# The first k-tile of a decoder trunk: its products term by term, and other idle matmuls ahead of them

## The chip, the cores and the metric

The kernel runs on one core of one Trainium2 chip. The metric is the device time of one execution in microseconds (us), as a median over runs. PE is TensorE, DVE VectorE, ACT ScalarE, POOL GpSimd and SP SyncE. PEld is PE's loading of weights, which overlaps its matmuls.

## The reference

The computation is a decoder trunk of two layers on 256 tokens of width 1024, in float32. Layer 0 mixes tokens by block attention with 16 heads of 64; with 256 tokens there is one block, so it is plain causal attention. Layer 1 mixes by dilated windows with 12 heads. Each mixer is followed by a dense MLP of width 4096 with a squared ReLU, and each of the four sub-layers by a layer norm.

```python
h = x
for i in range(DEPTH):                      # DEPTH = 2
    mix = moba_attention(...) if i % 2 == 0 else dilated_attention(...)
    h = layer_norm(DEEPNORM_ALPHA * h + mix, ln_mix_g[i], ln_mix_b[i])
    h = layer_norm(DEEPNORM_ALPHA * h + sq_relu_mlp(h, mlp_w_in[i], mlp_w_out[i]), ln_mlp_g[i], ln_mlp_b[i])
```

What matters here is the very first product, `qkv = x @ w_qkv` of layer 0, and of it the columns of the queries and keys.

## The kernel before, in words

Every float32 operand is split into a high and a low part of the type fp32r. A product is then three matmuls ("terms"): high weights by high tokens (term 0), high weights by low tokens (term 1), low weights by high tokens (term 2). ACT or DVE makes the high part (`whi`, `xs` part 0), DVE subtracts it from the source for the low part (`wlo`, `xs` part 1); both are done by `split` (lines 349 to 357).

The first block of work computes six weight tiles of 128 query and key columns (`NFIRST = 6`) over a contraction of 1024, which is cut into eight k-tiles of 128. One k-tile is a `Stage`: its 256 token columns and its 768 weight columns lie side by side in one array in DRAM, `xw0`, and are loaded together. `STAGE_PARTS` (line 54) says in how many parts a stage is loaded and split. The first k-tile has the tokens, then three parts of the weights: tile 0, tiles 1 and 2, tiles 3 to 5. SP loads the tokens with tile 0, ACT's queue loads the other five tiles. DVE makes the high part of tile 0, ACT the high parts of the other two. The second k-tile has two parts, tiles 0 and 1 and tiles 2 to 5; the later ones have fewer.

`Stage.mms(ps, j, term)` adds one matmul of weight tile `j` and one term: the weights are stationary (128x128), 256 token columns move. Two tiles share a PSUM bank, so the block uses three banks, `first_ps`. A k-tile has 18 of these matmuls, the block 144. The loop over the stages that the diff touches adds them, for the first k-tile in an order of its own: the three terms of tile 0 first, then term by term the tiles 1 to 5.

Ahead of the block stand idle matmuls: products of constant ones in bf16 into a bank that nobody reads. `WARM` (line 60) lists their column counts. One more idle matmul is added behind the first product of the first k-tile; it reads the same operands as that product, so that it cannot come sooner.

```python
def idle(n, reads=()):
    ones = nc.const_aps.tensor
    op("PE", n / 2400, lambda: mm(idle_ps.t[:, :n], ones(1.0, [P, P], BF16), ones(1.0, [P, n], BF16), True, True),
       list(reads), [idle_ps])
for n in WARM:
    idle(n)
```

The order on each engine is not the order of the program text. `op` only records an operation with its engine, an estimated cost, its reads and its writes. `Plan.order` (line 163) goes over the list twice. The first pass, in the order of the text, gives each operation a due time from PE's progress and the estimated arrivals of the loads. The second pass places operations engine by engine: of those that can start first, the one that is due first. SP's loads keep the order of the text. `Plan.emit` then writes the instructions in the order found. All matmuls show line 360 in the profile, the splits 351, 353 and 356, the loads 347; rows are told apart by their tiles.

Of the kernel before, what the change touches and what calls it, by code (L numbers as in the profile page):

```python
# [47 lines left out]
NFIRST = 6  # L48
# [8 lines left out]
    ((2, NFIRST), ("ACT", "ACT"), ((0, 1, "SP"), (2, 2, "SP"))),  # L57
    ((NFIRST,), ("ACT",), ((0, 1, "SP"),)),
)
WARM = (512,) * 6 + (384,)  # L60

# [51 lines left out]
class Plan:  # L115
# [16 lines left out]
    def op(self, eng, cost, fn, reads=(), writes=(), xfer=0.0, early=0.0, ahead=0.0):  # L132
        o = Op()
        o.n, o.eng, o.cost, o.fn, o.xfer = len(self.ops), eng, cost, fn, xfer
        o.early, o.ahead = early, ahead
        o.preds, o.succs, o.bufs = set(), [], set()
        for group, is_write in ((reads, False), (writes, True)):
            for item in group:
                b, key = item if isinstance(item, tuple) else (item, None)
                o.bufs.add(b)  # L140
                for k, st in b.state.items():
                    if key is None or k is None or k == key:
                        if st[0] is not None:
                            o.preds.add(st[0])
                        if is_write:
                            o.preds.update(st[1])
                st = b.state.setdefault(key, [None, []])
                if is_write:
                    if key is None:
                        b.state = {None: [o, []]}  # L150
                    else:
                        st[0], st[1] = o, []
                else:
                    st[1].append(o)
        o.preds.discard(o)
        for p in o.preds:
            p.succs.append(o)
        for b in o.bufs:
            b.left += 1
        self.ops.append(o)  # L160
        return o
# [129 lines left out]
def tile_trunk(  # L291
# [37 lines left out]
    def mk(shape, dt, tag, bufs, space=None):  # L329
        uid[0] += 1  # L330
        return plan.buf(Bufs(space or sb, bufs), shape, dt, tag, bufs, f"{tag}_{uid[0]}")

    def psum(tag):
        return mk([P, 512], F32, tag, 4, ps_pool)
# [24 lines left out]
    def mm(out_ap, lhsT, rhs, start, stop):  # L359
        nc.tensor.matmul(out_ap, lhsT, rhs, start=start, stop=stop)  # L360
# [16 lines left out]
    xs = [mk([P, 4, 2, S], F32R, f"xs{i}", 1) for i in range(2)]  # L377
# [73 lines left out]
    def idle(n, reads=()):  # L451
        ones = nc.const_aps.tensor
        op(
            "PE", n / 2400, lambda: mm(idle_ps.t[:, :n], ones(1.0, [P, P], BF16), ones(1.0, [P, n], BF16), True, True),
            list(reads), [idle_ps],
        )

    for n in WARM:
        idle(n)
# [140 lines left out]

    first_ps = [psum("acc") for _ in range(NFIRST // 2)]
    for st in stages:

        todo = sorted((st.kt + j > 0, term, j) for term in range(3) for j in range(NFIRST))
        for _, term, j in todo:
            st.mms(first_ps[j // 2], j, term)
            if st.kt == term == j == 0:
                idle(512, [(st.hi, (0, 1)), (xs[0], (0, 0, 0))])


    turns = {"score": 0, "prob": 0}
# [680 lines left out]
```

## Time and profile before

| | |
|---|---|
| time, median of 3 runs | 562.04 us (560.03, 562.04, 562.15) |
| profiled execution | 562.25 us |
| its span | 560.4 us |
| PE busy | 552.2 us (99% of the span) |
| PEld busy | 472.2 us (84%) |
| DVE busy | 412.3 us (74%) |
| ACT busy | 302.4 us (54%) |
| bytes moved by DMA | 105.60 MB, mean 188 GB/s |

A row of the timeline gives the start and the length in microseconds from the span's beginning, the engine, the line, the operation, what it writes and reads, the shape and how many instructions of a kind follow each other. The length of a merged row reaches to the end of its last instruction, and rows of matmuls overlap, so the pace of matmuls is read from the distance between starts. A bracket gives the idle time ahead of a row and what ended it.

### The profile page before, as it was taken

The page shows a single profiled execution, that of the slowest core. Times are in us where ns is not written, and L with a number is a line of the kernel's source. Part 1 is how long each engine was busy: PE and PEld are TensorE (multiplying, and loading weights), DVE is VectorE, ACT ScalarE, POOL GpSimd, SP SyncE. Part 2 cuts the span into 40 slices and gives each one's busy share as a digit, 9 for nine tenths or more (in the row PEclk, how much of TensorE's full clock was granted, in tenths as well). Part 3 has the DMA queues.
Part 4 walks back from the last instruction along what each step waited for, and adds up shares of the span by engine and source line. Part 5 has one row for each costly group of instructions (what it writes and reads, how often), then busy time and mean ns, then how long its engine had stood idle before and what let it go on. Part 6 is the DMA issues. An engine that isn't in the chain of part 4 may idle for free.

```text
span 560.4 us, 8584 instructions
## 1 busy us (share of the span) xinstructions
PE 552.2 (99%) x3235; PEld 472.2 (84%) x3235; DVE 412.3 (74%) x726; ACT 302.4 (54%) x491; POOL 8.6 (2%) x13
## 2 busy tenths in 40 slices
PE   9999999999999999999999999999999999999995
PEld 7988888888888888888888889888888888888884
DVE  6599999897764854855879999889848548458446
ACT  6367798258455455455534567545654554555400
POOL 0000000000000000000000000010000000000001
PEclk9999999999999999999999999999999999999998
DMA  8976145638885855647336535525877456463001
GB/s 334 404 280 207 51 167 198 235 112 299 268 272 157 245 171 186 225 153 223 123 141 216 198 118 185 169 94 181 300 233 252 163 187 224 149 227 113 1 0 75
DMA packets 30137, 105.60 MB, mean 188 GB/s; under 512 B 3345, under 2 KB 4113, under 8 KB 30097
## 3 DMA queue, kind: packets, MB, share of 16 engines
q1 hardware_dynamic: 29808, 104.48, 55.5%
q8 instruction: 25, 0.41, 0.3%
q10 hardware_dynamic: 288, 0.59, 0.3%
q14 instruction: 16, 0.12, 0.1%
HBM read 104.01 MB, written 1.05 MB: 187 GB/s over the span
## 4 chain that ended last, share of the span: by engine, by line
PE 98%; DMA 1%; DVE 0%; POOLq 0%; DVEq 0%; ACT 0%; issue 0%
PE acc L360 59%; PE tp L360 36%; PE tp L690 3%; DMA raw<-in_xw_dram 1%; POOLq L1286 0%; DVE tok L556 0%; DVEq L1286 0%; DVE bst L824 0%; ACT xs L351 0%; DVE mv L802 0%; DVE rstd L803 0%; POOLq L805 0%
## 5 line engine op out<-in xcount | busy, mean ns | idle before, releaser
L356 DVE TENSOR_TENSOR wlo<-raw,whi 128x1024 fp32r<-128x1024 f32 (+3 forms) x186 | 218.2, 1192 | 98.8 <-PE tp L360 53.1
L351 ACT ACTIVATE whi<-raw 128x1024 fp32r<-128x1024 f32 (+1 forms) x184 | 189.2, 1043 | 113.7 <-PE acc L360 68.5
L360 PE MATMUL acc<-whi,ahi 128*128 128x512 f32 (+1 forms) x312 | 121.6, 390 | 0.0
L360 PE MATMUL acc<-wlo,ahi 128*128 128x512 f32 (+1 forms) x312 | 121.0, 388 | 0.0
L360 PE MATMUL tp<-xs,whi 128*128 128x512 f32 x448 | 104.7, 390 | 0.0
L360 PE MATMUL acc<-whi,alo 128*128 128x512 f32 (+1 forms) x312 | 102.7, 387 | 0.0
L360 PEld LDWEIGHTS tp<-xs,whi 128*128 128x128 f32 x448 | 84.0, 188 | 17.3
L360 PEld LDWEIGHTS acc<-whi,alo 128*128 128x128 f32 x312 | 58.6, 188 | 12.1
L360 PEld LDWEIGHTS acc<-whi,ahi 128*128 128x128 f32 x312 | 58.7, 188 | 11.5 <-issue 0.3
L360 PEld LDWEIGHTS acc<-wlo,ahi 128*128 128x128 f32 x312 | 58.7, 188 | 11.2
L360 PE MATMUL acc<-xs,whi 128*128 128x512 f32 (+1 forms) x272 | 58.7, 364 | 0.6 <-ACT xs L351 0.6
L360 PEld LDWEIGHTS tp<-xs,wlo 128*128 128x128 f32 x448 | 55.6, 192 | 1.1
L360 PE MATMUL tp<-xs,wlo 128*128 128x256 f32 x448 | 55.9, 283 | 0.0
L360 PEld LDWEIGHTS acc<-xs,whi 128*128 128x128 f32 x272 | 46.0, 197 | 8.1 <-ACT xs L351 1.4
L351 ACT ACTIVATE ahi<-ta 128x256 fp32r<-128x256 f32 x56 | 23.5, 420 | 44.5 <-DVE ta L556 44.2
L913 ACT ACTIVATE ta<-tp 128x256 f32<-128x256 f32 x56 | 21.3, 381 | 26.2 <-PE tp L360 26.2
L549 DVE TENSOR_TENSOR ta<-tp,ta 128x256 f32<-128x256 f32 x56 | 23.5, 419 | 12.7 <-ACT ta L913 12.5
L360 PE MATMUL acc<-xs,wlo 128*128 128x256 f32 x224 | 31.4, 287 | 0.0
L360 PEld LDWEIGHTS acc<-xs,wlo 128*128 128x128 f32 x224 | 30.1, 196 | 1.0
L360 PE MATMUL acc<-whi,xs 128*128 128x512 f32 (+1 forms) x112 | 29.1, 367 | 0.0
L360 PE MATMUL tp<-whi,xs 128*128 128x512 f32 x80 | 25.2, 396 | 0.0
L556 DVE SCALAR_TENSOR_TENSOR ta<-ta 128x256 f32<-128x256 f32 x56 | 23.8, 425 | 1.8
(102 smaller groups left out, 464.3 us busy)
## 6 DMA issues: line engine op xcount, KB each, us to landing
raw<-in_win_dram SPq DMA_DIRECT2D x64, 512.0 KB, 4.3
raw<-in_wout_dram SPq DMA_DIRECT2D x64, 512.0 KB, 4.1
raw<-in_wqk_dram SPq DMA_DIRECT2D x22, 512.0 KB, 5.0
raw<-in_wo_dram SPq DMA_DIRECT2D x14, 512.0 KB, 4.3
raw<-in_wv_dram SPq DMA_DIRECT2D x8, 512.0 KB, 5.5
g<-in_lng_dram SPq DMA_DIRECT2D x4, 512.0 KB, 4.9
b<-in_lnb_dram SPq DMA_DIRECT2D x4, 512.0 KB, 6.2
raw<-in_wv1a_dram SPq DMA_DIRECT2D x4, 512.0 KB, 4.3
```

Source lines behind the costliest of these rows:

```text
L351: op("ACT", act(n, sbuf=sbuf), lambda: nc.scalar.activation(hi(), src(), AF.Copy), r, whi)
L356: lambda: nc.vector.tensor_tensor(lo(), src(), f32(hi()), op=ALU.subtract), list(r) + list(whi), wlo,
L360: nc.tensor.matmul(out_ap, lhsT, rhs, start=start, stop=stop)
L549: op("DVE", dve(n) + extra, lambda: nc.vector.tensor_tensor(out_ap(), a(), b(), op=alu), r, w)
L556: lambda: nc.vector.scalar_tensor_tensor(dst(), a(), s(), b(), op0=o0, op1=o1), r, w,
L690: nc.tensor.transpose(ps.t[:, c : c + P], src(), ident.t)
L913: op("ACT", act(S), lambda: nc.scalar.activation(u(), ps.t[:, S:], AF.Copy), [ps], uk)
```

## The change

Three things change. The idle matmuls at the beginning become eight of 512 columns; they were six of 512 and one of 384. The first k-tile's matmuls are added term by term, each term over all six weight tiles; before, tile 0 went through its three terms first. The one idle matmul behind the first product has 256 columns instead of 512. The other k-tiles were added term by term before and still are.

```diff
-WARM = (512,) * 6 + (384,)
+WARM = (512,) * 8
...
     first_ps = [psum("acc") for _ in range(NFIRST // 2)]
     for st in stages:
-
-        todo = sorted((st.kt + j > 0, term, j) for term in range(3) for j in range(NFIRST))
-        for _, term, j in todo:
-            st.mms(first_ps[j // 2], j, term)
-            if st.kt == term == j == 0:
-                idle(512, [(st.hi, (0, 1)), (xs[0], (0, 0, 0))])
+        for term in range(3):
+            for j in range(NFIRST):
+                st.mms(first_ps[j // 2], j, term)
+                if st.kt == term == j == 0:
+                    idle(256, [(st.hi, (0, 1)), (xs[0], (0, 0, 0))])
```

## The prediction

> **What bounds the kernel now.** I read the page first (busy shares and the chain), then busy time by stretches, then the timeline of the first 14 us, because all the edits lie there.
>
> ```profile
> span 560.4 us, 8584 instructions
> PE 552.2 (99%) x3235; PEld 472.2 (84%) x3235; DVE 412.3 (74%) x726; ACT 302.4 (54%) x491; POOL 8.6 (2%) x13
> PE 98%; DMA 1%; DVE 0%; POOLq 0%; DVEq 0%; ACT 0%; issue 0%
> ```
>
> ```profile
> 14.00:24.40 10.40, 10.40 (x89) 10.40 (x88) 4.46 (x6) 5.04 (x6) 0.00 (x0) 1.00 1.02 400
> 24.40:100.00 75.60, 75.60 (x596) 63.84 (x596) 72.59 (x180) 57.97 (x132) 0.00 (x0) 1.00 0.56 196
> 100.00:300.00 200.00, 200.00 (x1007) 170.04 (x1005) 138.94 (x203) 101.48 (x140) 3.88 (x4) 1.00 0.60 196
> 300.00:560.00 260.00, 253.48 (x1484) 217.51 (x1483) 186.96 (x320) 128.31 (x196) 3.96 (x4) 0.99 0.50 164
> ```
>
> The columns of the stretches are length, then busy time of PE, PEld, DVE, ACT and POOL, granted clock, DMA share and GB/s. PE has no idle time from 14 to 300 us, and the 6.5 us after that are about the tail behind its last matmul. So a microsecond that PE gains at the beginning should arrive at the end, if its data is there. The beginning itself:
>
> ```profile
> 0.77 3.04 PE L360 MATMUL tp<-const-bfloat16-1.0 128*128 128x512 bf16 x7 [0.77 <-PEq L1277]
> ...
> 2.43 0.15 PEld L360 LDWEIGHTS <-const-bfloat16-1.0 128*128 128x128 bf16 x1 [0.28 <-issue]
> 2.86 0.15 PEld L360 LDWEIGHTS <-const-bfloat16-1.0 128*128 128x128 bf16 x1 [0.28 <-issue]
> ...
> 4.37 0.58 PE L360 MATMUL acc<-xs,whi 128*128 128x256 f32 x1 [0.55 <-ACT xs L351]
> ...
> 4.75 0.65 PE L360 MATMUL tp<-const-bfloat16-1.0 128*128 128x512 bf16 x1
> ...
> 4.84 0.77 PE L360 MATMUL acc<-xs,whi 128*128 128x256 f32 x1
> ...
> 5.41 0.41 PE L360 MATMUL acc<-xs,wlo 128*128 128x256 f32 x1
> ...
> 5.62 2.33 PE L360 MATMUL acc<-xs,whi 128*128 128x256 f32 x10
> ...
> 7.76 1.27 PE L360 MATMUL acc<-xs,wlo 128*128 128x256 f32 x5
> ...
> 8.82 1.05 PE L360 MATMUL acc<-xs,whi 128*128 128x256 f32 x4
> ...
> 9.68 0.56 PE L360 MATMUL acc<-xs,wlo 128*128 128x256 f32 x2
> ...
> 10.07 1.11 PE L360 MATMUL acc<-xs,whi 128*128 128x256 f32 x8
> ...
> 11.02 0.64 PE L360 MATMUL acc<-xs,wlo 128*128 128x256 f32 x4
> ...
> 11.50 1.60 PE L360 MATMUL acc<-xs,whi 128*128 128x256 f32 x12
> ...
> 12.94 0.88 PE L360 MATMUL acc<-xs,wlo 128*128 128x256 f32 x6
> ```
>
> The starts give the pace. Ten products of 256 columns fill 5.62 to 7.76, or 0.213 us each; twelve fill 11.50 to 12.94, or 0.120 us each. The pace changes at about 10.0, inside the pair that starts at 9.68. The granted-clock column does not show this, but a halving of the array's clock fits it: 256 columns in 0.213 us are 1,200 a microsecond, and the idle matmuls of 512 columns start 0.43 us apart, the same rate. So PE ran slowly for its first 9.2 us, and 24 products (1, 1, 1, 10, 5, 4 and 2) ran before the fast pace. Each slow one costs 0.093 us more than a fast one. This stretch is what the change can move.
>
> Ahead of it lies a hole. The seventh idle matmul starts 0.43 behind the 2.86 of the sixth, at 3.29, and its 384 columns take 0.32, so the array is done at 3.61. The first product's row starts at 4.37; it lasts 0.58 where the slow row at 5.41 lasts 0.41, so its columns begin near 4.53. The hole is 0.76 by the rows, 0.92 by the columns. From 4.53 the array is never empty, and the fast pace comes about 5.5 us later.
>
> **The change, part by part.** *Eight idle matmuls of 512 instead of six and one of 384.* These are 640 columns more, 0.53 us at 1,200 a microsecond. They end at 4.14 instead of 3.61. The first product waits for its operand until 4.37, so the direct cost is nothing; the wait covers it with 0.23 to spare. Were the operand there at 3.61, the cost would be the full 0.53. I take zero, as the bracket of the 4.37 row names the wait. The hole shrinks to 0.23 by the rows, 0.39 by the columns.
>
> *The idle matmul behind the first product: 256 columns instead of 512.* It is on PE's path: 0.21 us less at the slow pace, 0.11 at the fast one.
>
> *The order.* The same 18 products of the first k-tile, each with its own weight load, go into the same three banks. Today the first weight tile's three terms come first; then the other five tiles. After the change the whole high-weight term comes first, so the second and third parts of the high weights are needed at once, and the low halves later. What hides this:
>
> ```profile
> 3.90 0.42 ACT L351 ACTIVATE xs<-raw 128x256 fp32r<-128x256 f32 x1 [0.96 <-DMA raw<-in_xw_dram]
> ...
> 4.16 0.29 DVE L356 TENSOR_TENSOR wlo<-raw,whi 128x128 fp32r<-128x128 f32 x1
> 4.22 0.81 ACT L351 ACTIVATE whi<-raw 128x256 fp32r<-128x256 f32 x2
> ...
> 4.37 0.42 DVE L356 TENSOR_TENSOR xs<-raw,xs 128x256 fp32r<-128x256 f32 x1
> ...
> 4.70 0.92 DVE L356 TENSOR_TENSOR wlo<-raw,whi 128x256 fp32r<-128x256 f32 x2
> ...
> 5.99 0.62 ACT L351 ACTIVATE whi<-raw 128x512 fp32r<-128x512 f32 x1
> ...
> 6.46 1.02 DVE L356 TENSOR_TENSOR wlo<-raw,whi 128x256 fp32r<-128x256 f32 x2
> ...
> 8.97 0.83 ACT L351 ACTIVATE whi<-raw 128x768 fp32r<-128x768 f32 x1
> ...
> 24.18 2.48 DVE L549 TENSOR_TENSOR ta<-acc,ropet 128x512 f32<-128x512 f32 x4 [5.11 <-PE acc L360]
> ```
>
> The first product's columns end at 4.53 + 0.21 = 4.74, the 256 idle ones at 4.96. The second product needs the second part of the high weights, the first half of ACT's pair from 4.22 to 5.03, so by about 4.65: 0.3 us to spare. The fourth needs the third part, 5.03, and comes at 4.96 + 0.43 = 5.39. The low half of the tokens (ready 4.79) is first used by the seventh product, the last low weights (5.62) by the sixteenth. So the order costs nothing, and without this cover PE would stand still by what the second part is late beyond 0.3 us. A gain from order alone is excluded: the number of products is the same and none waits today behind 4.84.
>
> *The other queues.* Operations are put on the engines by a planner in the kernel. No DMA, ACT or DVE operation is added, removed or resized. Only due times inside the first k-tile change. In the second k-tile PE takes 4, 2, 8 and 4 products (rows 8.82 to 11.02): the planner held back the later weight columns, so in its own reckoning PE waits for them. Such a wait ends at the same time whether PE came 0.1 us sooner or later, so what it decides behind it should stay. SP keeps the program's order of loads. I put this at zero.
>
> *The clock.* If the remaining hole of 0.23 to 0.39 us is too short to matter, PE's unbroken work begins with the idle matmuls at 0.77, not at 4.53. The slow pace lasted 5.5 to 5.6 us from the beginning of unbroken work; 0.77 + 5.6 is 6.4. The 25th product starts at 10.07 today. After the change the second starts at 4.96; 1.44 us remain until 6.4, which is 6.75 products at 0.213; 16.25 more at 0.120 take 1.95; the 25th starts at 8.35. That is 1.72 us sooner, the shorter idle matmul included.
>
> In the Trainium skill, "TensorE: Matmul & The Clock Gate", Part 1 ("What's actually happening"), the clock is raised at the end of a busy window of 3.413 us, and the windows run freely. An estimate by that page puts the boundary before 10.01 at 6.60, and the gain at 1.65 rather than 1.72. The trace agrees with such a grid:
>
> ```profile
> 556.00:556.10 0.10, 0.00 (x0) 0.00 (x0) 0.10 (x1) 0.00 (x0) 0.00 (x0) 1.00 0.00 0
> 556.10:556.20 0.10, 0.00 (x0) 0.00 (x0) 0.10 (x1) 0.00 (x0) 0.00 (x0) 0.73 0.00 0
> ```
>
> The granted clock falls near 556.15, and 556.15 - 10.01 is 160 of the page's windows.
>
> Bounds of the clock term: with the fast pace from the first product, the 25th starts at 4.53 + 0.12 + 0.11 + 23 x 0.12 = 7.52, 2.55 sooner. With the pace changing at 10 as now, only 0.21 is gained. I take 1.72, as the row nearest to it is the 5.5 us of this very trace.
>
> *Is the data there?* At 8.35 PE is in the second k-tile, which begins at 7.65 (the 19th product). Its high weights are done at 6.61, its last low weights at 7.48. The fourth begins 4.3 later, at 12.0; its high weights are done at 9.80. Behind the first block DVE stood idle for 5.11 us until 24.18, waiting for PE, so it starts sooner as well.
>
> *The sum.* The profiled execution took 562.25: a span of 560.4 and 1.85 around it. 562.25 - 1.72 = 560.5. It is 0.21 above the median 562.04, and from the median the result is 560.3.
>
> **The rivals.** *A: the hole is not what holds the clock back, or what remains of it still does.* Then the fast pace comes near 10 again and only the shorter idle matmul counts: 562.04 - 0.2 = 561.8. For it: no row tells how large a hole is harmless, and 0.39 is not nothing. Against it: the three times are 560.03, 562.04 and 562.15. A fast pace from the first product on, with today's 512 idle columns, would start the 25th product at 7.62 and end the profiled run at 562.25 - 2.45 = 559.8; the 560.03 lies close to that. So PE seems to rise early at times even with the large hole. The skill's same page ("Why this matters for your kernels") warns only of holes over about 3 us; by that rule neither hole would matter, and the time would be the 561.8 of this case. This trace shows a slow pace for 5.5 us behind a hole of 0.9, which speaks against the rule.
>
> *B: slower, the idle matmul has become too short.* It covered 0.43 us while the operands of the next product came; now it covers 0.21, and the next product needs a part that comes by the other load queue. If that part is over 0.3 us later than in this trace, PE runs empty there, and unbroken work begins only then. With 0.6 us more, the hole is 0.3 us, unbroken work begins at 5.26, and the fast pace comes 5.5 later, at 10.8 instead of 10.0: 0.8 us with 3.75 slow products, 0.35 us. With the hole and less the 0.21 that makes 562.04 + 0.44 = 562.5. Against it: both margins are 0.3 in the one trace that there is.
>
> *C: the gain is swallowed.* DVE is busy for 72.59 of the 75.60 us from 24.4 to 100. If it is the true bound there and its loads do not come sooner, PE waits again: 562.0. Against it: the 5.11 us that it waits for PE at 24.18.
>
> *D: the planner's order changes far behind the first k-tile.* That could go either way by some microseconds; for it speaks only that such lists are sensitive.
>
> **How the numbers follow.** The forecast has 0.70, with a range of its own from 559.5 (562.04 - 2.55) to 560.9 (the pace changing near 7.5). A has 0.16, B 0.06, C 0.04, D 0.04. Holding 8 in 10 needs the forecast and A: 559.3 to 562.0, with 0.2 us of scatter at both ends. Half a per cent, 2.8 us, is about what a measurement of this kernel can tell from no change. Faster by that means under 559.2, just beyond the earliest clock: 0.08, from scatter there and half of D. Slower by that means over 564.8, which only D or a large B reaches: 0.03. The rest is 0.89.
>
> **What would show it.** Right: eight idle rows from 0.77 whose last ends its columns near 4.14, the first product still at 4.37, the second at about 4.96 without a wait, and the pace changing from 0.213 to 0.120 between 4.4 and 7. From the second k-tile on the order of rows is the same, all some 1.7 us sooner, to the end. Wrong: the slow pace still there at 9 us (A), a wait on ACT's high weights behind the first product (B), an early pace but the same end (C), or a difference that grows after 30 us (D).

## The result, and the profile after

The changed kernel takes 560.12 us (median of 22 runs, 559.80 to 560.88) against 561.81 for the kernel before (22 runs, 559.80 to 562.47): 1.69 us less. The ratio is 0.9982, with a 95% interval of 0.9973 to 0.9990. The medians hide how the gain is made. Both kernels reach 559.80. The times of before fall into two groups with nothing between: 8 of the 22 runs lie at 559.80 to 560.21, the other 14 at 561.41 to 562.47. The changed kernel has no upper group. So the 1.69 depends on where the median of two groups happens to fall; in the mean of the 22 runs it is 1.08 us (561.31 to 560.23).

The page of the changed kernel, for its profiled execution of 560.12 us:

```profile
span 558.3 us, 8586 instructions
PE 550.3 (99%) x3236; PEld 470.0 (84%) x3236; DVE 412.1 (74%) x726; ACT 302.0 (54%) x491; POOL 8.6 (2%) x13
PE 98%; DMA 1%; DVE 0%; POOLq 0%; DVEq 0%; ACT 0%; issue 0%
```

PE is the bound as before, and busy 1.9 us less, though it has one instruction more. The timeline of its beginning:

```profile
0.77 3.57 PE L360 MATMUL tp<-const-bfloat16-1.0 128*128 128x512 bf16 x8 [0.77 <-PEq L1276]
...
4.59 0.41 PE L360 MATMUL acc<-xs,whi 128*128 128x256 f32 x1 [0.25 <-ACT xs L351]
...
4.84 0.28 PE L360 MATMUL tp<-const-bfloat16-1.0 128*128 128x256 bf16 x1
...
4.90 1.75 PE L360 MATMUL acc<-xs,whi 128*128 128x256 f32 x11
...
6.49 0.88 PE L360 MATMUL acc<-xs,wlo 128*128 128x256 f32 x6
...
7.21 0.64 PE L360 MATMUL acc<-xs,whi 128*128 128x256 f32 x4
...
7.68 0.40 PE L360 MATMUL acc<-xs,wlo 128*128 128x256 f32 x2
...
7.92 1.12 PE L360 MATMUL acc<-xs,whi 128*128 128x256 f32 x8
...
22.05 2.49 DVE L549 TENSOR_TENSOR ta<-acc,ropet 128x512 f32<-128x512 f32 x4 [1.58 <-PE acc L360]
```

The rows of ACT that the first products wait for:

```profile
4.12 0.42 ACT L351 ACTIVATE xs<-raw 128x256 fp32r<-128x256 f32 x1 [1.19 <-DMA raw<-in_xw_dram]
4.45 0.81 ACT L351 ACTIVATE whi<-raw 128x256 fp32r<-128x256 f32 x2
```

Among the products the slow pace is gone. The first product's row lasts 0.41 instead of 0.58, six products fill 6.49 to 7.21 (0.120 each), and the 25th product (behind 1, 11, 6, 4 and 2) starts at 7.92 instead of 10.07: 2.15 us sooner, although the first one came 0.22 later. The counts of the second k-tile, 4, 2, 8 and 4, are those of before. DVE's first rotation follows, at 22.05 instead of 24.18.

PE's last matmul, first in the timeline of before and then in that of the changed kernel:

```profile
553.20 0.28 PE L360 MATMUL tp<-whi,alo 128*128 128x256 f32 x1
```

```profile
551.09 0.28 PE L360 MATMUL tp<-whi,alo 128*128 128x256 f32 x1
```

From the 25th product to the last matmul it is 543.13 us before and 543.17 after. All that is won in the first 10 us arrives at the end, and nothing else is won. The same distance is 543.13 to 543.19 us in the profiles of the experiments below as well; only where the pace rose just behind the 25th product (the run with the order alone) is it 543.33. So the start of the 25th product tells a run's time.

The mark at which the granted clock falls after PE's last work has moved as well (in the stretches' rows the granted clock stands third from the end):

```profile
554.20:554.30 0.10, 0.00 (x0) 0.00 (x0) 0.10 (x2) 0.00 (x0) 0.00 (x0) 0.61 0.00 0
```

It falls at 554.22 (at 0.5 behind that point, 0.61 means a full clock for 0.02 of the 0.10 us). In the kernel before, the pace rose at 10.01 and the clock fell at 556.15, about 546.13 us later. The traces also hold the length of the stretch at the full clock: 546.132 us before, 549.546 in the changed kernel. These are 160 and 161 steps of 3.4133 us, the windows of 3.413 us that the prediction cites from the Trainium skill ("TensorE: Matmul & The Clock Gate", Part 1). So the clock of the changed kernel rose at 554.22 - 549.55 = 4.67, just behind the start of the first product. Below, "the grid" means this reckoning, the fall less 549.55; in the experiments it stands behind what the rows of matmuls show by themselves.

### The profile page after: what moved, and what is told of

Read it like the earlier page. It is cut to its first block, busy times and chain, and to the rows that moved or that the text cites. A ratio compares the mean times of both kernels' runs of the same rounds, so it can differ in the third digit from the quotient of the medians.

```text
span 558.3 us, 8586 instructions
## 1 busy us (share of the span) xinstructions
PE 550.3 (99%) x3236; PEld 470.0 (84%) x3236; DVE 412.1 (74%) x726; ACT 302.0 (54%) x491; POOL 8.6 (2%) x13
## 4 chain that ended last, share of the span: by engine, by line
PE 98%; DMA 1%; DVE 0%; POOLq 0%; DVEq 0%; ACT 0%; issue 0%
PE acc L360 59%; PE tp L360 36%; PE tp L689 3%; DMA raw<-in_xw_dram 1%; POOLq L1285 0%; DVE tok L556 0%; DVEq L1285 0%; DVE bst L823 0%; ACT xs L351 0%; DVE mv L801 0%; DVE rstd L802 0%; POOLq L804 0%
## 5 line engine op out<-in xcount | busy, mean ns | idle before, releaser
L360 PE MATMUL acc<-xs,whi 128*128 128x512 f32 (+1 forms) x272 | 56.8, 356 | 0.2 <-ACT xs L351 0.2
L360 PEld LDWEIGHTS acc<-xs,whi 128*128 128x128 f32 x272 | 44.4, 189 | 8.0 <-ACT xs L351 1.2
```

## The experiments

Two theories stood against each other. H: the hole between the last idle matmul and the first product decides whether the clock rises early. O: the order of the first k-tile and the shorter idle matmul bring the gain. A third, C, is told apart from H further on. In all eight kernels the work behind the first k-tile is the same. Each had 12 timed runs.

**Only the idle matmuls at the beginning.**

```diff
-WARM = (512,) * 6 + (384,)
+WARM = (512,) * 8
```

> Only the idle matmuls at the beginning are changed (eight of 512); order and the idle 512 behind the first product stay. Theory H (the hole between the last idle matmul and the first product decides when the fast pace comes; eight fill it down to about 0.4 us): as the changed kernel, plus 0.1 to 0.2 us for the 256 more idle columns: median 560.3, all runs between 559.8 and 561.3. Theory O (the order of the first k-tile and the shorter idle matmul bring the gain): as before, 561.8, with most runs above 561.3.

Measured: 560.39 us (559.79 to 561.23), ratio 0.9984 (0.9972 to 0.9997). On the same chip the kernel before had a median of 561.80. This edit alone brings nearly all of the gain, and it does away with the two groups: seven of the 12 runs lie in the stretch that before leaves empty on this chip, 560.23 to 561.51, and none above it. Its timeline, and the stretch in which the granted clock falls:

```profile
4.46 0.58 PE L360 MATMUL acc<-xs,whi 128*128 128x256 f32 x1
...
5.72 1.57 PE L360 MATMUL acc<-xs,whi 128*128 128x256 f32 x10
7.12 0.76 PE L360 MATMUL acc<-xs,wlo 128*128 128x256 f32 x5
```

```profile
555.70:555.80 0.10, 0.00 (x0) 0.00 (x0) 0.04 (x1) 0.00 (x0) 0.00 (x0) 0.57 0.80 307
```

Ten products fill 5.72 to 7.12, 1.40 us: two at 0.213 and eight at 0.120, so the pace rose near 6.2. The grid says 555.71 - 549.55 = 6.16.

**Only the order and the shorter idle matmul behind the first product.**

The changed kernel with the idle matmuls of before, so the edit is shown against the changed kernel:

```diff
-WARM = (512,) * 8
+WARM = (512,) * 6 + (384,)
```

> Only the order of the first k-tile and the idle 256 behind the first product are changed; the idle matmuls at the beginning stay six of 512 and one of 384. Theory H: as before less 0.1 to 0.2 us: median 561.6, in two groups (some runs below 560.3, most above 561.2). Theory O: as the changed kernel, 560.1, no run above 561.

Measured: 560.88 us, ratio 0.9997 (0.9981 to 1.0012); six runs at 559.82 to 560.14, six at 561.61 to 562.35. The median falls into the empty middle and says nothing; the two groups are those of before, at the same places (half of the 12 runs in the lower one, where before had 11 of 35 on the same chip; 12 runs can't tell these shares apart). The changed order does not do away with the upper group, and the run above does so without it: O has fallen. The profiled run is one of the upper group:

```profile
4.48 0.58 PE L360 MATMUL acc<-xs,whi 128*128 128x256 f32 x1 [0.67 <-ACT xs L351]
...
9.58 0.63 PE L360 MATMUL acc<-xs,wlo 128*128 128x256 f32 x2
10.00 1.21 PE L360 MATMUL acc<-xs,whi 128*128 128x256 f32 x8
```

The two products at 9.58 still take 0.42: slow until about 10.2.

**Five idle matmuls, a large hole.**

```diff
-WARM = (512,) * 6 + (384,)
+WARM = (512,) * 5
```

> The order stays as before. Five idle matmuls of 512 only: they end near 2.9 us and the hole is 1.6 us. Theory H: the early fast pace that some runs of before show (559.8 to 560.2) goes away altogether: all runs between 561.0 and 562.6, median 561.9, so 0.1 to 0.3 above before's median, with the low group gone. If the hole does not matter at all: the two groups of before, about a third of the runs below 560.3.

Measured: 561.95 us (561.27 to 562.52), ratio 1.0015 (1.0003 to 1.0028). The lower group of before is gone: none of 12 runs, where before had 11 of 35 on the same chip. The hole matters.

```profile
4.46 0.58 PE L360 MATMUL acc<-xs,whi 128*128 128x256 f32 x1 [1.39 <-ACT xs L351]
...
8.92 0.82 PE L360 MATMUL acc<-xs,whi 128*128 128x256 f32 x4
9.57 0.40 PE L360 MATMUL acc<-xs,wlo 128*128 128x256 f32 x2
```

PE stands idle for 1.39 us ahead of the first product. The four products from 8.92 to 9.57 take 0.65 us, two at 0.213 and two at 0.120: the pace rose near 9.3.

**Seven idle matmuls: how large a hole is harmless.**

```diff
-WARM = (512,) * 6 + (384,)
+WARM = (512,) * 7
```

> As before, but seven idle matmuls of 512: they end near 3.7 us and the hole is about 0.8 us by the columns (before 0.9, changed kernel 0.4). It tells how large a hole is harmless. Harmless up to about 0.85, as the third of early runs of before suggests: one group, 559.8 to 561.3, median 560.3. Harmless only up to less than 0.8: two groups as before, some 40% of the runs below 560.4 and the others above 561.2.

Measured: 560.26 us, ratio 0.9993 (0.9979 to 1.0007); seven runs at 559.94 to 560.38, five at 561.58 to 562.45. Two groups, so a hole of this size is not safe. But in the profiled run it did no harm:

```profile
0.77 3.15 PE L360 MATMUL tp<-const-bfloat16-1.0 128*128 128x512 bf16 x7 [0.77 <-PEq L1277]
4.36 0.58 PE L360 MATMUL acc<-xs,whi 128*128 128x256 f32 x1 [0.44 <-ACT xs L351]
...
5.62 1.40 PE L360 MATMUL acc<-xs,whi 128*128 128x256 f32 x10
6.85 0.76 PE L360 MATMUL acc<-xs,wlo 128*128 128x256 f32 x5
```

```profile
555.20:555.30 0.10, 0.00 (x0) 0.00 (x0) 0.10 (x1) 0.00 (x0) 0.00 (x0) 0.82 0.00 0
```

Ten products in 1.23 us: the pace rose near 5.7, and the grid says 555.26 - 549.55 = 5.71. The whole hole, from 3.71 to the first product's row at 4.36, 0.65 us, lies inside the 3.413 us ahead of that mark. In the profiled run of before the hole of 0.76, from 3.61 to 4.37, lies inside the 3.413 us ahead of 6.60, and there the clock did not rise. So what a step of the grid bears seems to lie between 0.65 and 0.76 us by the rows (0.81 and 0.92 by the columns), or about a fifth to a quarter of it. These are single runs; the first product began between 4.19 and 4.59 in the profiles, so the same kernel has a different hole from run to run.

**The same idle columns, but later.** Theory C says that not the hole counts but the number of idle columns, or the time since the first of them. The first attempt gave the first idle matmul a read of what GpSimd writes near 1.5 us, and six of 512:

```diff
-WARM = (512,) * 6 + (384,)
+WARM = (512,) * 6
...
+    for i, n in enumerate(WARM):
+        idle(n, [(warm, 1)] if i == 0 else [])
```

> The order stays as before. Six idle matmuls of 512, of which the first waits for the small GpSimd operation that ends near 1.5 us, so that they run from about 1.6 to 4.2: fewer idle columns than before (3,072 instead of 3,456), but the empty time lies ahead of them and the hole behind them is 0.4 us. Theory H: better than before, median about 560.6, runs spread from 559.8 to 561.4 without a gap. Rival C (the number of idle columns decides, or the time since the first one): no better than before, 561.8 to 562.2, and no low group.

Measured: 561.60 us, ratio 1.0001 (0.9986 to 1.0016), four runs at 559.84 to 560.23 and eight at 561.50 to 562.33. It did not do what was meant:

```profile
0.77 2.72 PE L360 MATMUL tp<-const-bfloat16-1.0 128*128 128x512 bf16 x6 [0.77 <-PEq L1277]
4.19 0.58 PE L360 MATMUL acc<-xs,whi 128*128 128x256 f32 x1 [0.70 <-ACT xs L351]
```

The idle matmuls began at 0.77: the reads that are given to `idle` only steer the planner, and make no instruction wait. (So it is by its place in the planned order, and not by a wait for what it is said to read, that the one idle matmul comes behind the first product.) The run is a control: six of 512 from 0.77 give two groups. The second attempt put a real wait ahead of the same six:

```diff
-WARM = (512,) * 6 + (384,)
+WARM = (512,) * 6
...
+    op("PE", 0.02, lambda: mm(idle_ps.t[:, :4], ones(1.0, [P, P], BF16), warm.t.bitcast(BF16), True, True),
+       [(warm, 0), (warm, 1)], [idle_ps])
     for n in WARM:
         idle(n)
```

> Six idle matmuls of 512 as in the run before that was meant to start late and did not; this time a matmul of 4 columns stands ahead of them that reads what GpSimd writes near 1.5 us, so that they run from about 1.7 to 4.3 us. Same idle columns, but the empty time lies ahead of them and the hole behind them is 0.2 us. Theory H (an almost unbroken stretch of about 3.4 us, ending at a mark of a fixed grid, brings the fast pace): the two groups merge into one, spread from 559.9 to 561.6, median about 560.8. Rival C (the number of idle columns, or the time since the first of them, decides): as the six that began at 0.77, two groups or only the high one, median 561.6 or more.

Measured: 560.29 us (559.93 to 561.12), ratio 0.9990 (0.9978 to 1.0001), one group. The interval touches 1 because that ratio is taken over before's two groups. Against the control the difference is 1.3 us in the median and all of the upper group, eight runs of 12 there and none here. The two ran on different chips, on which before had medians of 561.80 and 561.65.

```profile
1.58 0.16 PE L360 MATMUL tp<-warm,const-bfloat16-1.0 128*128 128x4 bf16 x1 [1.58 <-POOL warm L444]
1.60 2.72 PE L360 MATMUL tp<-const-bfloat16-1.0 128*128 128x512 bf16 x6
4.59 0.58 PE L360 MATMUL acc<-xs,whi 128*128 128x256 f32 x1 [0.27 <-ACT xs L351]
...
5.85 1.36 PE L360 MATMUL acc<-xs,whi 128*128 128x256 f32 x10
7.05 0.76 PE L360 MATMUL acc<-xs,wlo 128*128 128x256 f32 x5
```

The ten products from 5.85 take 1.20 us, so all of them run at the fast pace. Six idle matmuls that reach to 0.27 us before the first product's row (4.32, the end of their row) are worth more than six, or the seven of before, that begin 0.8 us earlier. C has fallen: it is the hole.

**Without the idle matmul behind the first product.** The edit is against the changed kernel.

```diff
-                if st.kt == term == j == 0:
-                    idle(256, [(st.hi, (0, 1)), (xs[0], (0, 0, 0))])
```

> The changed kernel without the idle matmul behind the first product. If that matmul only fills time in which PE would wait for the second part of the high weights: same as the changed kernel, 560.1, between 559.8 and 560.9. If it is on the path: 0.1 to 0.2 less, 559.9 to 560.0. If it keeps the clock up by filling a hole (rival B of the prediction): a high group above 561 comes back.

Measured: 560.11 us (559.84 to 560.71), ratio 0.9988 (0.9977 to 0.9999): the changed kernel's time without it.

```profile
4.31 2.06 PE L360 MATMUL acc<-xs,whi 128*128 128x256 f32 x12
6.21 0.88 PE L360 MATMUL acc<-xs,wlo 128*128 128x256 f32 x6
6.93 0.64 PE L360 MATMUL acc<-xs,whi 128*128 128x256 f32 x4
7.41 0.40 PE L360 MATMUL acc<-xs,wlo 128*128 128x256 f32 x2
7.65 1.12 PE L360 MATMUL acc<-xs,whi 128*128 128x256 f32 x8
```

From the first product to the 25th it is 3.34 us (4.31 to 7.65), in the changed kernel 3.33 (4.59 to 7.92). The twelve products from 4.31 take 1.90 us, where 0.120 each would be 1.44. So the idle matmul fills time in which PE waits for the second and third part of the weights anyway.

**Useful products in that place.** Here the other two terms of tile 0 follow its first product, the low weights first, and there is no idle matmul behind it. The edit is against the changed kernel.

```diff
-        for term in range(3):
-            for j in range(NFIRST):
-                st.mms(first_ps[j // 2], j, term)
-                if st.kt == term == j == 0:
-                    idle(256, [(st.hi, (0, 1)), (xs[0], (0, 0, 0))])
+        todo = [(term, j) for term in range(3) for j in range(NFIRST)]
+        if st.kt == 0:
+            lead = [(0, 0), (2, 0), (1, 0)]
+            todo = lead + [x for x in todo if x not in lead]
+        for term, j in todo:
+            st.mms(first_ps[j // 2], j, term)
```

> Eight idle matmuls of 512, none behind the first product; in the first k-tile the two other terms of the first weight tile follow its first product (low weights first, whose operand is ready earlier), then the rest term by term. Theory: in runs with an early fast pace PE waits for the second and third part of the high weights in the changed kernel (starts 0.2 us apart instead of 0.12); two useful products in that place save 0.2 to 0.4 us: median 559.8 to 559.9, range 559.5 to 560.7. If the loads behind set the pace anyway: 560.1 as the changed kernel.

Measured: 560.18 us (559.79 to 560.60), ratio 0.9982 (0.9971 to 0.9994). It does not beat the changed kernel.

```profile
0.77 3.32 PE L360 MATMUL tp<-const-bfloat16-1.0 128*128 128x512 bf16 x8 [0.77 <-PEq L1277]
4.57 0.39 PE L360 MATMUL acc<-xs,whi 128*128 128x256 f32 x1 [0.48 <-ACT xs L351]
4.79 0.30 PE L360 MATMUL acc<-xs,wlo 128*128 128x256 f32 x1
5.05 1.56 PE L360 MATMUL acc<-xs,whi 128*128 128x256 f32 x11
...
7.77 1.12 PE L360 MATMUL acc<-xs,whi 128*128 128x256 f32 x8
```

```profile
4.58 0.42 DVE L356 TENSOR_TENSOR xs<-raw,xs 128x256 fp32r<-128x256 f32 x1
```

```profile
553.20:553.30 0.10, 0.00 (x0) 0.00 (x0) 0.10 (x1) 0.00 (x0) 0.10 (x1) 0.76 0.00 0
```

From the first product to the 25th it is 3.20 us (4.57 to 7.77), 0.13 less than in the changed kernel, and not the 0.2 to 0.4 expected: the third product needs the low half of the tokens, which DVE finishes only at 5.00, and starts at 5.05. Where the clock's mark falls moves the time by 0.8 us from run to run, so 12 runs don't show 0.13.

## Why the prediction was right, and where it was not

**The sum.** 560.3 was forecast for the median, 560.12 came out. For the profiled execution the forecast was 1.72 us less and 2.13 were found (562.25 to 560.12). The mechanism was the one forecast: the smaller hole lets the clock rise earlier. The mis-sized term is when it rises. I let the fast pace come 5.6 us after the beginning of unbroken work, at 6.4; in this trace it came at 4.7, 3.9 us after the first idle matmul. Two misses in the other direction took back part of that: against 7.52, the prediction's own bound for a fast pace from the first product, the 25th product came 0.40 later. The operand came 0.22 later, and PE waited some 0.27 for weights (below); why the two are 0.09 more than the 0.40 stays open. One number of the prediction is slightly off: its own steps give 1.63, not 1.65, for a boundary at 6.60.

**The step that failed** is the constant of 5.5 us. There is none. The pace rose at 4.7 in the changed kernel and near 6.2 and 5.7 in the kernels with only eight and with seven idle matmuls, which all began them at 0.77; with five it rose near 9.3, 4.9 us after the first product's row began. What fits all of these is the rule of the Trainium skill, "TensorE: Matmul & The Clock Gate", Part 1 ("What's actually happening"), to which the prediction gave only a sentence: windows of 3.413 us that run freely, of which a busy one raises the clock. The traces agree: the stretch at the full clock is 160 steps (546.132 us) or 161 (549.546) in each of the ten. In the table, the rise is the fall of the granted clock less that stretch, and "mark" is the first step of the grid behind the whole hole. The holes are by the rows, from the end of the last idle matmul's columns to the first product's row.

| kernel | hole, us | mark behind it | clock falls | clock rises |
|---|---|---|---|---|
| no idle matmul behind the first product | 0.17 | 4.45 | 553.99 | 4.45 |
| only the eight idle matmuls | 0.32 | 6.16 | 555.71 | 6.16 |
| changed kernel | 0.45 | 4.67 | 554.22 | 4.67 |
| six, begun later | 0.48 | 5.87 | 555.41 | 5.87 |
| seven | 0.65 | 5.71 | 555.26 | 5.71 |
| before | 0.76 | 6.60 | 556.15 | 10.01 |
| only the order | 0.87 | 6.77 | 556.31 | 10.18 |
| six | 0.90 | 6.54 | 556.08 | 9.95 |
| five | 1.60 | 5.91 | 555.45 | 9.32 |

In these profiles the clock rises, with a hole of up to 0.65, at the mark behind it, with 0.76 and more only at the next one. In the tenth, with useful products in the place of the idle matmul, a mark lay at 3.70, ahead of the hole, and the clock rose there. The kernel's start falls anywhere on that grid, so every run draws its own mark: with the same eight idle matmuls the rise came at 3.70, 4.45, 4.67 and 6.16. The changed kernel's runs are spread over 1.08 us; at 0.093 us lost in each 0.213 of slow pace that is about 2.5 us between the earliest rise that matters and the latest (an estimate; only one of these runs has a trace). That the forecast of the median was close is partly luck: 6.4 is a late draw beside these four, and the 562.04 from which it was taken off was the median of three runs of which two happened to be in the upper group.

**The groups.** My argument against rival A, that the 560.03 of before was a run whose clock rose early in spite of the hole, has held, as far as the runs show: before has a lower group in a third of the cases, and five idle matmuls take it away. In the traces of the upper group the window with the hole is lost and the clock rises a whole window later. No run of before's lower group was profiled. The profile of seven idle matmuls is the only one of a lower group; its hole was borne. That a mark inside the hole can also split it, so that each window has only a part, would fit but is not shown.

**Eight idle matmuls cost nothing:** right. The first product still waits for its operand (0.25 us). It began at 4.59, not at 4.37, since the operand came 0.22 later in that run; ACT, and not PE, is named as the releaser (its row for the tokens begins at 4.12, in the kernel before at 3.90).

**The shorter idle matmul, 0.21:** nearly right at the slow pace (0.18), nothing at the fast one. With only order and idle matmul changed, the first product to the 25th took 5.52 us (4.48 to 10.00) where before took 5.70 (4.37 to 10.07). In the changed kernel's early clock, leaving it out altogether changes nothing.

**The order costs nothing:** not quite. I worked out the margins of 0.3 us at the slow pace. At the fast pace they are used up: the eleven products from 4.90 to 6.49 take 1.59 us, where 0.120 each would be 1.32. So 0.27 us go into waiting for the second and third part of the weights; ACT ends that pair at 5.26 (4.45 + 0.81), and the fourth product is the first to need the third part. The run with useful products in that place got 0.13 of it back.

**The other queues and the data:** right. The work behind the first k-tile kept its order, and the distance from the 25th product to the end is the same to 0.04 us. Rival C is excluded by that. Its cover has shrunk, though: DVE's wait for PE ahead of the rotation is 1.58 us now, 5.11 before.

**Rival B** did not come up. Without any idle matmul behind the first product no run was above 560.71; the waits among its first twelve products add up to 0.46 us (1.90 less 1.44), under the 0.65 us that a window bore. **Rival D** did not come up either.

**Against taking it that only holes of over 3 us count:** the row of the Trainium skill ("TensorE: Matmul & The Clock Gate", "Why this matters for your kernels") that warns of holes over about 3 us is about drops in mid-kernel. Here a hole of 0.76 us cost a window before the clock had risen, and with one of 1.6 us none of 12 runs had the early clock. For the first rise that row is no guide.

What stays open: how exactly a window is judged. All nine profiles of the table fit a boundary between 0.65 and 0.76 us, but the two ends rest on one profile each, and these two kernels have runs in both groups.

## What to carry to other kernels

Idle matmuls that raise PE's clock are worth what they do to the hole ahead of the first real product: let them reach up to it, and count the hole, not the matmuls. Where times fall into groups, look at which group the profiled run belongs to, and compare groups and not medians. Margins that were worked out at the slow pace must be worked out again at the fast one.

## What the runs showed of the hardware that was not expected

The clock can rise before the first real product. In the run with useful products in the place of the idle matmul, the eight idle matmuls fill 3.32 us instead of 3.57, the first product's row lasts 0.39 instead of 0.58, and the grid says 553.25 - 549.55 = 3.70. A hole of about 0.8 us ahead of the first product kept PE at half its pace for 3.4 us more in the traces of the upper group, which costs about 1.5 us (an estimate: 16 products at 0.213 instead of 0.120).
